# A delta-rule mixer: the chunk decay goes from the keys to the values, its state product becomes two half products on opposite rows, and the gate's projections are issued during the inversions

## The chip, the cores and the metric

The kernel runs on one core of a Trainium2 chip, in one launch. The figure of merit is the device time of one execution in microseconds (us); the median of the runs is given. Beside these times stands one profiled execution, whose trace gives the rows below.

## The reference, cut to what matters

A first block (mixer, then 32 experts) is followed by a second block. The change touches only the first block's mixer, which works on 256 context and 256 latent tokens of width 1024. It has a gated delta rule of 8 heads and a gated linear attention (GLA) of 4 heads, both run forwards and backwards:

```
def step(s, xs_n):                       # delta rule, chunks of 64 tokens
    u_n, w_n, attn_n, qg_n, kd_n, gl_n = xs_n
    v_new = u_n - w_n @ s
    o_n = qg_n @ s + attn_n @ v_new
    s = s * gl_n + kd_n^T @ v_new        # kd = k * exp(g[-1] - g)
    return s, o_n

ya = (rms_norm(o_a) * silu(za)) @ w_out_a      # za: columns 3072..4095 of the input projection
yb = (rms_norm(o_b) * silu(rb)) @ w_out_b
y  = (sigmoid(gates_a) * ya + sigmoid(gates_b) * yb) @ w_out
```

`u` and `w` come from a unit lower triangular system per chunk. `kd` scales every key row (token) of a chunk by its decay to the chunk's end. Since the product sums over tokens, the same factor may stand on the rows of `v_new`.

## The kernel before, in words

The mixer is `phase1`. Its program order around the change is written out as a string, `DELTA_ORDER` (L187), one letter for a piece of work: `K`, `Q`, `V` take a 128-column tile of keys, queries or values through projection, convolution and norm (`P` starts such a tile ahead); `M` forms the triangular systems of four heads; nine `X` are the steps of their inversion (`inverses`, L630 and L632: a product and a subtraction on VectorE per row, 31 rows); `H` prepares a head (`head_setup`); eight `S` scan a pair of heads (`scan_step`); `k`, `q`, `v` project GLA's keys, queries and values; `m` computes a part of the modulation (`fill_mod`, eight 1 MB pieces of `w_mod`). `GLA_ORDER` does the same behind it: there `S` forms a quarter of the delta branch's norm and gate, and `silu_cols` in it projects 256 columns of `za`. A scheduler then interleaves the engines' instructions by its own costs; each engine and each queue works through its list in order.

Forward and backward chunks share every tile: at step n the forward chunk `cf` sits on one half of the 128 rows (`rf`) and the backward chunk `cb` on the other (`rb`), and the halves swap with every step. Per head and step, `scan_step` does this:

- L717, L718: keys times state, two products of 64 rows of output, into the two halves of one PSUM tile; L720: `r`, on VectorE.
- L723: `vn`, the inverse times `r`.
- L725, L726: `vn` is copied by ScalarE into the two diagonal blocks of `vb`, a 128x256 tile whose other blocks GpSimd has set to zero (L701).
- L741: one product of the scaled keys `ks` with `vb`, 256 columns wide, so that each half of the rows meets only its own columns.
- L743, or L745 and L747: the new state of both directions.
- from step 4 on L730, L731, L733, L735 to L737: the outputs.

`ks` is made in `head_setup`: `scaled` (L694) multiplies the keys in token order by `eDL`, on GpSimd, as it multiplies the values by `Bt` on VectorE. Both are four instructions a head. Three of the buffers named `y` by the trace (pool `p1y`, three of them, 8 KB a partition) hold a pair's `TT`, `vs` and `ks`; the pieces of `w_mod` pass through the same three.

A projection (`proj_tm`) has its weights split into a high and a low part by ScalarE (L150) and VectorE (L151), and three fp32r products for each of the eight row tiles of the weight (L164). For `za` there are two token tiles of 256 columns per letter `S`, and VectorE reads each from PSUM (L880).

Of the kernel before, what the change touches and what calls it, by code (L numbers as in the profile page):

```python
# [9 lines left out]
F32 = mybir.dt.float32  # L10
# [3 lines left out]
ALU = mybir.AluOpType  # L14
# [178 lines left out]
def phase1(k, A, B):  # L193
# [28 lines left out]
    def chps():  # L222
        return ps.tile([128, 128], F32, name=k.nm("ch"), tag="ch", bufs=3)

# [310 lines left out]
    def fill_gv(h):  # L535
        t = wd.tile([128, 4, 256], F32, name=k.nm("gv"), tag="gv", bufs=2)
        proj_tm(w_in[:, 5152 + h * 256:5408 + h * 256], range(4), hTh, hTl, lambda i, o: nc.scalar.copy(t[:, i, :], o))
        gv.append(t)

    msc = k.dpool.tile([4, 1024], F32, name="msc")  # L540
    k.msc = msc

    def fill_mod(j):
        mp = ps.tile([128, 512], F32, name=k.nm("ch"), tag="ch", bufs=3)
# [8 lines left out]
    fills = {"k": fill_gk, "q": fill_gq, "v": fill_gv}  # L553

# [93 lines left out]

    def head_setup(h, TT, vs, ks):
        hh, h, (M, EA, Dn, Dt) = h, h % 4, groups[h // 4]  # L650
# [46 lines left out]
        comb(vs, scaled(nc.vector, vts[hh], Bt))  # L697
        comb(ks, scaled(nc.gpsimd, kt, eDL))
        st = wd.tile([128, 256], F32, name=k.nm("st"), tag="st", bufs=2)
        vb = wd.tile([128, 2, 256], F32, name=k.nm("vb"), tag="vb", bufs=2)  # L700
        nc.gpsimd.memset(vb, 0.0)  # L701
        os_ = wd.tile([128, 4, 128], F32, name=k.nm("os"), tag="os", bufs=2)
        return A2, TT, vs, ks, st, vb, os_

    def scan_step(p, n):
# [5 lines left out]
        for h in hs:  # L711
            A2, TT, vs, ks, st, vb, os_ = sets[h]
            if n == 0:
# [25 lines left out]
            if n < 7:  # L739
                pu = ps.tile([128, 256], F32, name=k.nm("pu"), tag="pu", bufs=1)  # L740
                nc.tensor.matmul(pu, ks[:, n, :], vq, start=True, stop=True)  # L741
                if n == 0:
                    nc.vector.tensor_copy(st, pu)  # L743
                else:
                    nc.vector.scalar_tensor_tensor(st[:, 0:128], st[:, 0:128], gl[:, h, cf:cf + 1],  # L745
                                                   pu[:, 0:128], op0=ALU.mult, op1=ALU.add)
                    nc.vector.scalar_tensor_tensor(st[:, 128:256], st[:, 128:256], gl[:, 8 + h, cb:cb + 1],  # L747
                                                   pu[:, 128:256], op0=ALU.mult, op1=ALU.add)
        if n < 7:
# [10 lines left out]
    for c in DELTA_ORDER:  # L760
# [8 lines left out]
        elif c in "KQV":  # L769
            ct = order.pop(0)  # L770
            x = conv_silu(ct)
            if c == "K":
                kT = wd.tile([128, 512], F32, name=k.nm("kT"), tag="kT", bufs=5)
                l2n(x, 512, kT, 0.0)
                kTs.append(kT)
            elif c == "Q":
                qT = wd.tile([128, 256], F32, name=k.nm("qT"), tag="qT", bufs=4)
                l2n(x, 256, qT, qbias)
                qTs.append(qT)
            else:  # L780
# [20 lines left out]
    def gla_gates(h, d):  # L801

        f = d == 0
        kT, qT = gk[h], gq[h]
        pz = ps.tile([128, 512], F32, name=k.nm("ch"), tag="ch", bufs=3)
        nc.tensor.matmul(pz, gw[32 * d:32 * d + 16, h * 128:(h + 1) * 128], lr[32 * d:32 * d + 16, :], start=True, stop=True)
        T2 = lambda nm, tag, b=2: (wd if tag == "kt" else wk).tile([128, 512], F32, name=k.nm(nm), tag=tag, bufs=b)
        z, l = T2("z", "acc"), T2("l", "e", 3)
# [60 lines left out]
        p1 = ps.tile([128, 256], F32, name=k.nm("pu"), tag="pu", bufs=1)  # L869
# [4 lines left out]
    def silu_cols(c0, dst, ccs=range(4)):  # L874

        for cc in ccs:
            def ev(t, o):
                d = dst[t - 2][:, cc * 256:cc * 256 + 256]
                x = wk.tile([128, 256], F32, name=k.nm("zx"), tag="Z", bufs=2)
                nc.vector.tensor_scalar_max(x, o, LOW)  # L880
                sigmoid(k, d, x)
                nc.vector.tensor_mul(d, x, d)
            proj_tm(w_in[:, c0 + cc * 256:c0 + cc * 256 + 256], (2, 3), hTh, hTl, ev)

# [65 lines left out]
    for c in GLA_ORDER:  # L950
# [1105 lines left out]
```

## Time and profile before

| | us |
|---|---|
| median of 3 runs | 2509.11 |
| lowest and highest | 2506.01, 2515.05 |
| the profiled execution | 2497.63 |
| its span on the core | 2495.8 |
| busy in it: PE (TensorE) | 2326.6 (93%) |
| busy: DVE (VectorE) | 1236.1 (50%) |
| busy: ACT (ScalarE) | 920.5 (37%) |
| busy: POOL (GpSimd) | 117.9 (5%) |

The page's 40 slices show three parts: the mixer up to about 745 us, the experts from 760 to 1700 us (DMA at nine tenths or more), and the second block to the end. The mixer's stages, read from the first and last starts of their lines: first inversion 107 to 176 us; scan of pair 0 to 222; its setup for pair 1 to 240; pair 1 to 285; second inversion and setup 300 to 367; pair 2 to 410; setup of pair 3 to 429; pair 3 to 467; GLA and the gates to 640; output projections and router to 745. A share of busy time over the whole span says little here: each stage has its own limit, so the windows by stage are the view to read.

### The profile page before, as it was taken

How to read it: one execution, taken by the hardware profiler on the slowest of the kernel's cores; microseconds unless marked ns; L12 is line 12 of the kernel's file. 1: busy time of each engine (PE TensorE's matmuls, PEld its weight loads, DVE VectorE, ACT ScalarE, POOL GpSimd, SP SyncE). 2: the span in 40 equal slices, each digit the busy share in tenths (PEclk: the TensorE clock that was granted, in tenths of full speed). 3: DMA queues.
4: the chain of work that ended last, by engine and by line, in shares of the span. 5: the costliest groups of instructions: out<-in, count | busy, mean ns of one | idle time of the engine just before them, and what ended most of it. 6: DMA issues, size and time to landing. Idle time of an engine off the chain costs nothing.

```text
span 2495.8 us, 36511 instructions
## 1 busy us (share of the span) xinstructions
PE 2326.6 (93%) x14474; PEld 1567.1 (63%) x14475; DVE 1236.1 (50%) x2717; ACT 920.5 (37%) x1956; POOL 117.9 (5%) x156
## 2 busy tenths in 40 slices
PE   6689879999989999999899999999999999999998
PEld 3476557889873433333334333336868999878998
DVE  4898897677560111112202121115766556766655
ACT  4556555577430101010101010104555445455544
POOL 0122122000010000000000000000010000010000
PEclk8899988999999999999999999999999999999999
DMA  8532330234889999999999999995335554524553
GB/s 285 139 85 60 133 97 26 60 94 120 283 297 380 415 416 416 416 416 416 389 416 415 416 415 416 416 415 150 112 85 173 170 171 155 159 73 138 186 186 102
DMA packets 290349, 605.90 MB, mean 243 GB/s; under 512 B 26038, under 2 KB 218681, under 8 KB 254332
## 3 DMA queue, kind: packets, MB, share of 16 engines
q1 hardware_dynamic: 283236, 595.24, 64.9%
q10 hardware_dynamic: 6280, 7.80, 1.2%
q8 instruction: 116, 1.90, 0.3%
q0 software_dynamic: 656, 0.46, 0.1%
q14 instruction: 61, 0.50, 0.1%
HBM read 602.30 MB, written 1.15 MB: 242 GB/s over the span
## 4 chain that ended last, share of the span: by engine, by line
PE 25%; issue 14%; DMA 9%; DVE 2%; ACT 1%; POOL 0%; SPq 0%; POOLq 0%; DVEq 0%; ACTq 0%
PE qm L164 13%; DMA w<-in_w_gu_dram 6%; PE yd L1373 2%; DMA w<-in_w_down_dram 2%; PE gt L1357 2%; PE lt L1357 2%; PE tr L1342 1%; PE qm L1789 0%; PE qm L1788 0%; PE ql L1852 0%; POOL bs L1805 0%; PE ql L1614 0%; PE tr L1286 0%; PE lt L1362 0%; PE gt L1362 0%
## 5 line engine op out<-in xcount | busy, mean ns | idle before, releaser
L150 ACT CAST wh<-w 128x1024 fp32r<-128x1024 f32 (+2 forms) x318 | 318.6, 1002 | 298.3 <-PE qm L164 201.2
L151 DVE TENSOR_TENSOR wl<-w,wh 128x1024 fp32r<-128x1024 f32 (+2 forms) x318 | 370.2, 1165 | 38.4 <-ACT wh L150 36.8
L1252 ACT ACTIVATE sg<-g 128x1024 f32<-128x1024 f32 x16 | 16.9, 1057 | 726.9 <-DVE g L1250 682.2
L164 PE MATMUL qm<-uh,wh 128*128 128x272 f32 (+2 forms) x1008 | 260.2, 292 | 0.0
L164 PE MATMUL qm<-ul,wh 128*128 128x272 f32 (+2 forms) x1008 | 258.3, 289 | 0.0
L1250 DVE TENSOR_SCALAR g<-gt 128x1024 f32<-128x1024 f32 x16 | 19.6, 1225 | 469.0 <-PE gt L1362 413.5
L1373 PE MATMUL yd<-w,aT 128*64 128x512 f32 x1024 | 228.3, 600 | 0.2 <-ACT aT L1264 0.2
L164 PEld LDWEIGHTS qm<-uh,wh 128*128 128x128 f32 (+1 forms) x1008 | 188.8, 188 | 7.4 <-issue 5.1
L164 PEld LDWEIGHTS qm<-ul,wh 128*128 128x128 f32 (+1 forms) x1008 | 189.3, 188 | 2.5 <-issue 0.7
L1357 PE MATMUL lt<-w,resB 128*64 128x512 f32 x512 | 189.6, 594 | 0.6 <-DVE act L1251 0.6
L1357 PE MATMUL lt<-w,xg 128*64 128x512 f32 x512 | 188.2, 596 | 0.0
L1357 PE MATMUL gt<-w,resB 128*64 128x512 f32 x512 | 182.6, 599 | 5.5 <-DMA w<-in_w_gu_dram 5.5
L1357 PE MATMUL gt<-w,xg 128*64 128x512 f32 x512 | 177.1, 602 | 8.5 <-DMA w<-in_w_gu_dram 8.3
L1373 PEld LDWEIGHTS yd<-w,aT 128*64 128x64 f32 x1024 | 72.9, 138 | 143.2 <-issue 140.8
L164 PE MATMUL qm<-uh,wl 128*128 128x272 f32 (+2 forms) x1008 | 147.7, 287 | 0.0
L1272 DVE TENSOR_TENSOR ys<-yd,g2r 128x512 f32<-128x512 f32 x32 | 20.6, 686 | 248.0 <-PE yd L1373 231.4
L164 PE MATMUL mm<-hTh,wh 128*128 128x256 f32 (+1 forms) x384 | 130.1, 358 | 8.3 <-ACT wh L150 4.1
L164 PEld LDWEIGHTS qm<-uh,wl 128*128 128x128 f32 (+1 forms) x1008 | 132.4, 187 | 0.7 <-issue 0.4
L164 PE MATMUL qm<-fl,wh 128*128 128x272 f32 (+1 forms) x512 | 128.6, 287 | 0.0
L164 PE MATMUL qm<-fh,wh 128*128 128x272 f32 (+1 forms) x512 | 128.4, 288 | 0.0
L164 PE MATMUL mm<-hTl,wh 128*128 128x256 f32 (+1 forms) x384 | 125.8, 347 | 0.0
L1357 PEld LDWEIGHTS lt<-w,xg 128*64 128x64 f32 x512 | 60.0, 138 | 71.4 <-issue 70.1
(581 smaller groups left out, 4392.7 us busy)
## 6 DMA issues: line engine op xcount, KB each, us to landing
w<-in_w_gu_dram SPq DMA_DIRECT2D x256, 1024.0 KB
w<-in_w_down_dram SPq DMA_DIRECT2D x128, 1024.0 KB
w<-in_w_ff_dram SPq DMA_DIRECT2D x64, 1024.0 KB
w<-in_w_in_dram SPq DMA_DIRECT2D x72, 512.0 KB
w<-in_w_in_dram SPq DMA_DIRECT2D x30, 1024.0 KB
y<-in_w_mod_dram SPq DMA_DIRECT2D x19, 1024.0 KB
w<-in_w_out_dram SPq DMA_DIRECT2D x24, 512.0 KB
w<-in_w_mod_dram SPq DMA_DIRECT2D x5, 1024.0 KB
```

The costliest lines, as they stand in the source:

```text
L150: k.nc.scalar.copy(hi, x)
L151: k.nc.vector.tensor_sub(lo, x, hi.bitcast(F32))
L164: nc.tensor.matmul(out, l, r, start=start and n == 1, stop=stop and n == 3 * len(terms))
L1250: nc.vector.tensor_scalar(g, gt, 7.0, LOW / 1.702, op0=ALU.min, op1=ALU.max)
L1252: nc.scalar.activation(sg, g, AF.Exp, scale=-1.702)
L1272: nc.vector.tensor_mul(ys[:, js], yd[:, js], g2r[:, js])
L1342: nc.tensor.matmul(o, hx[:, t, f * 128:(f + 1) * 128], S[t].rearrange("p e s -> p (e s)"), start=(t == 0 and i == 0), stop=(t == 1 and i = ...
L1357: nc.tensor.matmul(quarter(j)[64 * i:64 * i + 64], xg[:, kk, c0:c0 + CAP], w[i][:, j * 512:(j + 1) * 512], start=(kk == 0), stop=False)
L1373: nc.tensor.matmul(yd[64 * i:64 * i + 64, j * 512:(j + 1) * 512], aT[:, 2 * f2 + f, 64 * i:64 * i + 64], w[i][:, f, j * 512:(j + 1) * 512] ...
```

## The change

Part one moves the decay. `eDL` is combined once into `ceDL` (four VectorE copies), and `scan_step` writes the scaled `vn` in one ScalarE activation with a scale per row. `ks`, its 32 GpSimd products and the zeroing of `vb` go; at the last step, where no state follows, the copies go too.

Part two splits the state product by rows. The two halves of the keys `kt` and of `vq` are multiplied in two products over 64 rows each, into two PSUM tiles. `ch` has four buffers where it had three, and the tag `pu` goes.

Part three takes the four `za` projections out of GLA's `S` and gives them a letter of their own, `s`, after the third and sixth `X` of each inversion. Their result now holds one of the three `y` buffers from then on; a pair's setup needs two.

```diff
-DELTA_ORDER = "EkPPKPKPKPKMmXXXXXXXXXPQPQPVVHHkqSSSSSSSS...EkPPKPKPKPKMXXXXXXXXXPQPQPVmVHHSSSSSSSS..."
+DELTA_ORDER = "EkPPKPKPKPKMmXXXsXXXsXXXPQPQPVVHHkqSSSSSSSS...EkPPKPKPKPKMXXXsXXXsXXXPQPQPVmVHHSSSSSSSS..."
-        return ps.tile([128, 128], F32, name=k.nm("ch"), tag="ch", bufs=3)
+        return ps.tile([128, 128], F32, name=k.nm("ch"), tag="ch", bufs=4)
+    comb(ceDL, lambda r, d, q: nc.vector.tensor_copy(d, tv(eDL[:, :, 8 * q:8 * q + 8])[r]))
+    def fill_z(i):
+        if i == 0:
+            t = big([2, 1024])
+            z.extend(t[:, j, :] for j in range(2))
+        silu_cols(3072, z, (i,))
...
-        comb(ks, scaled(nc.gpsimd, kt, eDL))
-        vb = wd.tile([128, 2, 256], F32, name=k.nm("vb"), tag="vb", bufs=2)
-        nc.gpsimd.memset(vb, 0.0)
+        vb = wd.tile([128, 2, 128], F32, name=k.nm("vb"), tag="vb", bufs=2)
...
-            vq = vb[:, u]
-            nc.scalar.copy(vq[rf, 0:128], vn[rf])
-            nc.scalar.copy(vq[rb, 128:256], vn[rb])
+            if n < 7:
+                vq = vb[:, u]
+                nc.scalar.activation(vq, vn, AF.Copy, scale=ceDL[:, n, h:h + 1])
...
-                nc.tensor.matmul(pu, ks[:, n, :], vq, start=True, stop=True)
+                pu = chps(), chps()
+                nc.tensor.matmul(pu[0], kt[rf, cf // 2, :], vq[rf], start=True, stop=True)
+                nc.tensor.matmul(pu[1], kt[rb, cb // 2, :], vq[rb], start=True, stop=True)
...
-                trio = [big([2, 8, 128]) for _ in range(3)]
+                duo = [big([2, 8, 128]) for _ in range(2)]
-        G = T2("G", "kt")
+        G = T2("G", "vt")
-        p0 = ps.tile([128, 256], F32, name=k.nm("pu"), tag="pu", bufs=1)
+        p0 = ps.tile([128, 256], F32, name=k.nm("pu"), tag="ch", bufs=4)
...
             ba_.rms(2 * i, 2)
-            silu_cols(3072, z, (i,))
             ba_.columns(i)
```

TensorE's list in the scan of pair 3, before (`vb` the copied values, `y` the scaled keys, `st` the state, `kT` keys, `tm` a projection with weight parts `wh`, `wl`):

```order
L164 MATMUL tm_4540<-wh_4523,hTl 128x256
L164 MATMUL tm_4540<-wh_4523,hTh 128x256
L164 MATMUL tm_4540<-wh_4523,hTl 128x256
L735 MATMUL ch_4212<-vn_734_4210,A_680_3949 128x128
L741 MATMUL pu_4216<-vb_4021,y_677_3941 128x256
L717 MATMUL ch_4220<-st_4102,kT_2719 64x128
L718 MATMUL ch_4220<-st_4102,kT_2719 64x128
L164 MATMUL tm_4540<-wl_4524,hTh 128x256 x4
```

And in the scan of pair 3 of the changed kernel (`vb` the scaled values, `kt` the plain keys in token order):

```order
L164 MATMUL tm_4833<-wh_4829,hTh 128x256
L762 MATMUL ch_4454<-vb_4321,kt_4251 128x128
L763 MATMUL ch_4455<-vb_4321,kt_4251 128x128
L737 MATMUL ch_4460<-st_4397,kT_2875 64x128
L738 MATMUL ch_4460<-st_4397,kT_2875 64x128
L164 MATMUL tm_4833<-wh_4829,hTl 128x256
L164 MATMUL tm_4833<-wl_4830,hTh 128x256 x4
```

The wide product has become two neighbours of half its width, directly ahead of the other head's keys-times-state pair; that holds for 47 of the 56 state products.

VectorE's list near the end of the first inversion, before (`Ts`, `tmp` the inversion, `acc` a convolution tap, `wl` a weight's low part):

```order
L632 TENSOR_TENSOR Ts_969<-Ts_969,tmp_972 128x8x24
L151 TENSOR_TENSOR wl_1157<-w_1154,wh_1156 128x1024
L630 TENSOR_TENSOR tmp_972<-Ms_967,Ts_969 128x175
L501 SCALAR_TENSOR_TENSOR acc_1130<-pad_1127,cwT,acc_1130 128x256
L632 TENSOR_TENSOR Ts_969<-Ts_969,tmp_972 128x7x25
L515 TENSOR_TENSOR qT_1088<-e_1082,e_1089 128x256
L630 TENSOR_TENSOR tmp_972<-Ms_967,Ts_969 128x156
L501 SCALAR_TENSOR_TENSOR acc_1130<-pad_1127,cwT,acc_1130 128x256
L632 TENSOR_TENSOR Ts_969<-Ts_969,tmp_972 128x6x26
```

At the same rows of the inversion, changed (`zx` the evicted quarter of `za`, L652 and L654 the inversion):

```order
L654 TENSOR_TENSOR Ts_974<-Ts_974,tmp_977 128x8x24
L652 TENSOR_TENSOR tmp_977<-Ms_972,Ts_974 128x175
L151 TENSOR_TENSOR wl_1096<-w_1093,wh_1095 128x1024
L549 TENSOR_SCALAR zx_1057<-tm_1001 128x256
L654 TENSOR_TENSOR Ts_974<-Ts_974,tmp_977 128x7x25
L652 TENSOR_TENSOR tmp_977<-Ms_972,Ts_974 128x156
L654 TENSOR_TENSOR Ts_974<-Ts_974,tmp_977 128x6x26
L652 TENSOR_TENSOR tmp_977<-Ms_972,Ts_974 128x135
L654 TENSOR_TENSOR Ts_974<-Ts_974,tmp_977 128x5x27
L151 TENSOR_TENSOR wl_1128<-w_1125,wh_1127 128x1024
L551 TENSOR_TENSOR y_112_994<-zx_1057,y_112_994 128x256
```

The gate's work has taken the place of convolution taps (L501) between the inversion's rows; the taps stand later in the list.

GpSimd's list ahead of the scan of pair 3, before (`y` at L668 the tile `TT`, at L694 the scaled keys):

```order
L668 MEMSET y_675_3939 128x1024 x2
L701 MEMSET vb_4021 128x512
L654 MEMSET A_680_3949 128x512
L701 MEMSET vb_4103 128x512
L654 MEMSET A_692_4031 128x512
L694 TENSOR_TENSOR y_677_3941<-kt_3947,tok 64x4x128
L694 TENSOR_TENSOR y_677_3941<-kt_3947,tok 64x2x2x128
L694 TENSOR_TENSOR y_677_3941<-kt_3947,tok 64x4x128
```

And the same place, changed:

```order
L676 MEMSET A_759_4253 128x512
L690 MEMSET y_755_4244 128x1024 x2
L676 MEMSET A_771_4330 128x512
L879 MEMSET AT_4993 128x256
L879 MEMSET AT_5054 128x256
```

The products on the keys are gone from GpSimd's list, and GLA's zeroing (L879) follows at once.

## Rows read from the trace of the kernel before

**Rows 1.** Windows by stage: us, busy time and instructions per engine, granted clock, DMA share, GB/s.

```profile
107.00:176.00 69.00, 51.29 (x375) 39.70 (x367) 65.68 (x135) 35.85 (x78) 13.65 (x13) 0.90 0.39 108
176.00:222.00 46.00, 45.99 (x278) 32.85 (x278) 37.22 (x97) 27.20 (x76) 4.21 (x6) 0.97 0.16 47
...
300.00:367.00 67.00, 50.81 (x342) 32.64 (x341) 61.65 (x142) 31.45 (x72) 12.45 (x14) 0.87 0.37 119
410.00:429.00 19.00, 12.97 (x179) 10.09 (x179) 15.01 (x26) 13.18 (x49) 13.43 (x14) 0.71 0.01 2
429.00:467.00 38.00, 38.00 (x262) 30.23 (x261) 17.22 (x51) 14.33 (x46) 0.00 (x0) 0.97 0.15 42
467.00:640.00 173.00, 170.04 (x1245) 153.95 (x1245) 134.35 (x328) 124.41 (x309) 2.50 (x8) 1.00 0.40 115
...
760.00:1700.00 940.00, 879.80 (x3782) 341.23 (x3779) 165.44 (x238) 87.54 (x124) 1.09 (x2) 0.99 1.00 406
```

**Rows 2.** Windows, L164 on PE alone, in the GLA stage: us, busy, clock, DMA, GB/s.

```profile
467.00:640.00 173.00, 126.49 (x972) 1.00 0.40 115
```

**Rows 3.** Timeline of PE in the scan of pair 3: start, us, instruction, count.

```profile
454.74 0.28 PE L164 MATMUL tm<-wh,hTl 128*128 128x256 f32 x1
454.86 0.28 PE L164 MATMUL tm<-wh,hTh 128*128 128x256 f32 x1
...
456.35 0.59 PE L741 MATMUL pu<-vb,y 128*128 128x256 f32 x2
456.78 0.38 PE L735 MATMUL ch<-vn,A 128*128 128x128 f32 x2
457.10 0.32 PE L717 MATMUL ch<-st,kT 128*64 128x128 f32 x1
```

**Rows 4.** Timeline of PE in the second block, around products over 64 rows.

```profile
1731.97 0.29 PE L164 MATMUL qm<-uh,wh 128*128 128x272 f32 x1
1732.19 0.51 PE L1720 MATMUL ql<-ki,resA 64*128 64x144 f32 x2
1732.63 0.39 PE L164 MATMUL qm<-ul,wh 128*128 128x272 f32 x1
...
1736.24 0.52 PE L1720 MATMUL ql<-ki,resA 64*128 64x144 f32 x4
1736.69 0.39 PE L164 MATMUL qm<-uh,wh 128*128 128x272 f32 x1
```

**Rows 5.** One line's instructions, L694 on DVE: count, ns shortest/median/longest, first and last start.

```profile
L694 DVE TENSOR_TENSOR y<-vt,tok x32: 673/690/1541, 156.1 to 428.9; 64x512 f32<-64x512 f32 x32
```

**Rows 6.** Groups by shape, 60 to 480 us: busy us, mean ns; idle before, releasers.

```profile
L151 DVE TENSOR_TENSOR wl<-w,wh 128x1024 fp32r<-128x1024 f32 x36 | 43.8, 1217 | 5.1 <-ACT wh L150 3.8 <-PE mm L164 1.2
L694 POOL TENSOR_TENSOR y<-kt,tok 64x512 f32<-64x512 f32 x32 | 38.8, 1230 | 26.6 <-ACT kt L646 25.0 <-PE ch L723 1.0
...
L694 DVE TENSOR_TENSOR y<-vt,tok 64x512 f32<-64x512 f32 x32 | 30.9, 985 | 0.3
...
L726 ACT COPY vb<-ch 64x128 f32<-64x128 f32 x64 | 16.7, 260 | 0.8
...
L755 DVE TENSOR_TENSOR resB<-os 64x256 f32<-64x256 f32 x16 | 10.1, 633 | 0.2
```

**Rows 7.** Timeline of DVE in the setup of pair 3: start, us, instruction, count.

```profile
414.45 0.85 DVE L755 TENSOR_TENSOR resB<-os 64x256 f32<-64x256 f32 x2
...
417.00 1.44 DVE L694 TENSOR_TENSOR y<-vt,tok 64x512 f32<-64x512 f32 x1
418.36 2.45 DVE L755 TENSOR_TENSOR resB<-os 64x256 f32<-64x256 f32 x2
420.83 4.35 DVE L694 TENSOR_TENSOR y<-vt,tok 64x512 f32<-64x512 f32 x3
...
426.24 3.32 DVE L694 TENSOR_TENSOR y<-vt,tok 64x512 f32<-64x512 f32 x4
```

**Rows 8.** One line's instructions, L880: the eviction of the gate's projection.

```profile
L880 DVE TENSOR_SCALAR zx<-tm x16: 409/416/426, 478.5 to 620.4; 128x256 f32<-128x256 f32 x16
```

More of the change, by code (lines that the diff above doesn't have):

```diff
@@ L181, in parts @@
     return wh, wl
-DELTA_ORDER = "EkPPKPKPKPKMmXXXXXXXXXPQPQPVVHHkqSSSSSSSSPPQPQPVVHHSSSSSSSSEkPPKPKPKPKMXXXXXXXXXPQPQPVmVHHSSSSSSSSkPPQPQPVqqVHHSSSSSSSSqvv"
+DELTA_ORDER = "EkPPKPKPKPKMmXXXsXXXsXXXPQPQPVVHHkqSSSSSSSSPPQPQPVVHHSSSSSSSSEkPPKPKPKPKMXXXsXXXsXXXPQPQPVmVHHSSSSSSSSkPPQPQPVqqVHHSSSSSSSSqvv"
 GLA_ORDER = "DSGGGGOvDSGODGSORvDSRGRBBBGbORbbBbbbbb"
@@ L459, in phase1 @@
     ceG = one.tile([128, 8, 8], F32, name="ceG")
+    ceDL = one.tile([128, 8, 8], F32, name="ceDL")
     comb(cnbe, lambda r, d, q: nc.vector.tensor_copy(d, tv(nbe[:, :, 8 * q:8 * q + 8])[r]))
     comb(ceG, lambda r, d, q: nc.vector.tensor_copy(d, tv(eG[:, :, 8 * q:8 * q + 8])[r]))
+    comb(ceDL, lambda r, d, q: nc.vector.tensor_copy(d, tv(eDL[:, :, 8 * q:8 * q + 8])[r]))
     pcw = smps(216)
@@ L538, in fill_gv, with silu_cols, ev @@
         gv.append(t)
+    def silu_cols(c0, dst, ccs=range(4)):
+        for cc in ccs:
+            def ev(t, o):
+                d = dst[t - 2][:, cc * 256:cc * 256 + 256]
+                x = wk.tile([128, 256], F32, name=k.nm("zx"), tag="Z", bufs=2)
+                nc.vector.tensor_scalar_max(x, o, LOW)
+                sigmoid(k, d, x)
+                nc.vector.tensor_mul(d, x, d)
+            proj_tm(w_in[:, c0 + cc * 256:c0 + cc * 256 + 256], (2, 3), hTh, hTl, ev)
     msc = k.dpool.tile([4, 1024], F32, name="msc")
@@ L543, in fill_mod @@
     def fill_mod(j):
-        mp = ps.tile([128, 512], F32, name=k.nm("ch"), tag="ch", bufs=3)
+        mp = ps.tile([128, 512], F32, name=k.nm("ch"), tag="ch", bufs=4)
         for kk in range(8):
@@ L551, in fill_mod @@
                                 mo[32 * q:32 * q + 1, :])
-    fills = {"k": fill_gk, "q": fill_gq, "v": fill_gv}
+    z = []
+    def fill_z(i):
[3 more added lines that the diff above has]
+        silu_cols(3072, z, (i,))
+    fills = {"k": fill_gk, "q": fill_gq, "v": fill_gv, "s": fill_z}
     groups, kTs, qTs, vts, sets = {}, [], [], [], {}
@@ L647, in to_tok, with head_setup @@
         return vt
-    def head_setup(h, TT, vs, ks):
+    def head_setup(h, TT, vs):
         hh, h, (M, EA, Dn, Dt) = h, h % 4, groups[h // 4]
@@ L697, in head_setup @@
         comb(vs, scaled(nc.vector, vts[hh], Bt))
-        comb(ks, scaled(nc.gpsimd, kt, eDL))
         st = wd.tile([128, 256], F32, name=k.nm("st"), tag="st", bufs=2)
-        vb = wd.tile([128, 2, 256], F32, name=k.nm("vb"), tag="vb", bufs=2)
-        nc.gpsimd.memset(vb, 0.0)
+        vb = wd.tile([128, 2, 128], F32, name=k.nm("vb"), tag="vb", bufs=2)
         os_ = wd.tile([128, 4, 128], F32, name=k.nm("os"), tag="os", bufs=2)
-        return A2, TT, vs, ks, st, vb, os_
+        return A2, TT, vs, kt, st, vb, os_
     def scan_step(p, n):
@@ L711, in scan_step @@
         for h in hs:
-            A2, TT, vs, ks, st, vb, os_ = sets[h]
+            A2, TT, vs, kt, st, vb, os_ = sets[h]
             if n == 0:
@@ L739, in scan_step @@
             if n < 7:
-                pu = ps.tile([128, 256], F32, name=k.nm("pu"), tag="pu", bufs=1)
-                nc.tensor.matmul(pu, ks[:, n, :], vq, start=True, stop=True)
[L742 to L748, printed above, removed]
+                pu = chps(), chps()
+                nc.tensor.matmul(pu[0], kt[rf, cf // 2, :], vq[rf], start=True, stop=True)
+                nc.tensor.matmul(pu[1], kt[rb, cb // 2, :], vq[rb], start=True, stop=True)
+                for d, c in enumerate((cf, cb)):
+                    sd = st[:, 128 * d:128 * d + 128]
+                    if n == 0:
+                        nc.vector.tensor_copy(sd, pu[d])
+                    else:
+                        nc.vector.scalar_tensor_tensor(sd, sd, gl[:, 8 * d + h, c:c + 1], pu[d], op0=ALU.mult, op1=ALU.add)
         if n < 7:
@@ L787, in phase1 @@
             if i % 2 == 0:
-                trio = [big([2, 8, 128]) for _ in range(3)]
-            sets[i] = head_setup(i, *(x[:, i % 2] for x in trio))
+                duo = [big([2, 8, 128]) for _ in range(2)]
+            sets[i] = head_setup(i, *(x[:, i % 2] for x in duo))
         elif c == "S":
@@ L804, in gla_gates @@
         kT, qT = gk[h], gq[h]
-        pz = ps.tile([128, 512], F32, name=k.nm("ch"), tag="ch", bufs=3)
+        pz = ps.tile([128, 512], F32, name=k.nm("ch"), tag="ch", bufs=4)
         nc.tensor.matmul(pz, gw[32 * d:32 * d + 16, h * 128:(h + 1) * 128], lr[32 * d:32 * d + 16, :], start=True, stop=True)
-        T2 = lambda nm, tag, b=2: (wd if tag == "kt" else wk).tile([128, 512], F32, name=k.nm(nm), tag=tag, bufs=b)
+        T2 = lambda nm, tag, b=2: (wd if tag == "vt" else wk).tile([128, 512], F32, name=k.nm(nm), tag=tag, bufs=b)
         z, l = T2("z", "acc"), T2("l", "e", 3)
@@ L868, in gla_gates @@
         nc.scalar.copy(ss_[:, 0, :], p0)
-        p1 = ps.tile([128, 256], F32, name=k.nm("pu"), tag="pu", bufs=1)
+        p1 = ps.tile([128, 256], F32, name=k.nm("pu"), tag="ch", bufs=4)
         nc.tensor.matmul(p1, kdt[:, 2, :], gv[h][:, 2 + fi, :], start=True, stop=True)
@@ L872, in gla_gates @@
         return qs, AT, ss_
[L874 to L883, printed above, removed]
     def gate_cols(base, dst, tiles=range(8)):
@@ L930, in columns @@
                                                op0=ALU.mult, op1=ALU.subtract)
-    z, ga = big([2, 1024]), big([8, 256])
-    z, ga = [z[:, t, :] for t in range(2)], [ga[:, i, :] for i in range(8)]
+    ga = big([8, 256])
+    ga = [ga[:, i, :] for i in range(8)]
     ba_ = Branch(oa, 8, z, 32, Halves(wk, k, "g4", 2), Halves(wk, k, "s16", 2))
@@ L1039, in ev_out @@
         return fn
-    pl = [ps.tile([128, 32], F32, name=k.nm("pl"), tag="ch", bufs=3) for _ in range(2)]
+    pl = [ps.tile([128, 32], F32, name=k.nm("pl"), tag="ch", bufs=4) for _ in range(2)]
     def logits(cc):
```

## The prediction, made before the changed kernel ran

> **What bounds the kernel now.** I read the slices of the page first: three parts, of which only the mixer (to 745 us) holds edited code. The window over the experts shows DMA busy for 1.00 of 940 us at 406 GB/s [rows 1], and the second block is unchanged. Both start from what the mixer hands over, so I count a microsecond saved in the mixer as one saved in all, and nothing saved behind it.
>
> Next came the windows by stage [rows 1]. They show three kinds. In the inversions (107 to 176, 300 to 367) DVE is busy for 65.68 of 69 and 61.65 of 67 us, while PE leaves 17.7 and 16.2 us idle: DVE sets the time. In the scans (176 to 222, 429 to 467) PE is busy throughout, 45.99 of 46 and 38.00 of 38, and DVE leaves 8.8 us in the first. In the GLA stage PE is busy for 170.04 of 173 us against 134.35 on DVE, and 126.49 of it are projections [rows 2]. So the same microsecond of PE costs nothing in an inversion and a whole one in the GLA stage, and a microsecond of DVE the reverse. The setup before pair 3 (410 to 429) is short of either: its path is a chain, and 13.43 of its 19 us have GpSimd busy.
>
> Third were the shapes of L694 and what DVE does beside it [rows 5 to 7].
>
> **The change part by part.** Terms are on the profiled execution, 2497.63 us.
>
> *GpSimd's products go.* They are 32 of 1230 ns, 38.8 us on GpSimd [rows 6]. GpSimd's own time I leave out: the setup of pair 3 ends with DVE's products (426.24 + 3.32, so 429.56 [rows 7]), not with GpSimd. What counts is DVE beside them. L694 on DVE takes 690 ns in the median and 673 at the least, but 985 in the mean [rows 5, 6]: 32 x (985 - 690) = 9.4 us lost. L755 takes 0.85 us for two when undisturbed and 2.45 in the midst of it [rows 7], 633 ns in the mean [rows 6] against 425: 16 x 0.208 = 3.3. Together 12.7 us. Other DVE operations must meet the same products, so the true relief is larger: if all 38.8 us took from DVE what L755 lost at 418.36 (1.225 against 0.425, 65%), it would be 25. Against that, part of it lies where a chain waits for PE or ACT. In the setup of pair 3 it can be followed [rows 7]: eight products take 1.44 + 4.35 + 3.32 = 9.1 us where 8 x 0.69 = 5.5 would do, and the L755 pair loses 1.6, so up to 5.2 us of that stretch. I take the 12.7 that rows show, -13, with -25 and -5 as ends.
>
> The Trainium skill would have it larger for each meeting ("SBUF — State Buffer", Who interferes with whom): a DVE instruction with both inputs in SBUF and a GpSimd one that reads SBUF exclude each other, and the loser waits the whole instruction. By that, some 15 disturbed products at 1.2 us each would give 18 us where the means give 9.4. The longest L694 on DVE, 1541 ns against 690 [rows 5], is 0.85 over: less than a whole GpSimd product. I stay with the means.
>
> *The gate's projections in the inversions.* A quarter costs DVE two weight splits of 1.217 [rows 6], two evictions of 0.416 [rows 8] and two multiplications that I price alike: 4.1 us, four quarters 16.4. The inversions are where DVE is full. But the order shows that convolution taps left the inversion's last rows for later in the list, and behind it come the scans, where DVE idles 8.8 of 46 us. About half should be absorbed: +9, from 0 to +16. On PE a quarter is 2 x 8 x 3 = 48 products, and those follow each other by 0.12 us (454.74 to 454.86, [rows 3]): 192 x 0.12 = 23 us, against 33.9 us of idle PE in the two inversions. Hidden there; if the evictions come late it is not, which is the slow rival below.
>
> *The same work out of the GLA stage.* PE loses 23 of its 170 us, DVE 16.4 of 134, so PE is still the bound (147 against 118). The 3 us that PE idles now stay: -22. From below, DVE or a chain of ScalarE takes over halfway, -11; from above, some waits at evictions go as well, -27.
>
> *The state product in two halves.* Before, L741 stands 0.43 us (456.35 to 456.78, [rows 3]). There is no such product over 64 rows in the mixer, but there is one in the second block: L1720, a 64-row product of 144 columns. One (x2 records) takes 0.44 us to the next start, two (x4) take 0.45 (1736.24 to 1736.69, [rows 4]): the two lie beside each other at no added time. From the projected end of the neighbour before it (1731.97 + 0.12) to the start of the one behind (1732.63) are 0.54 us. Its entry alone is 0.10 (1732.09 to 1732.19), and I take its exit alike, which leaves 0.34 for the product, 0.30 at 128 columns. In 47 of 56 places the next instruction is L717, a product over the columns' halves, whose own entry was paid before too. So the pair costs 0.10 + 0.30 = 0.40 against 0.43 there, and 0.50 against 0.43 in the nine others: 47 x -0.03 + 9 x 0.07 = -0.8. The state update is two small copies for one at n = 0 and waits on two PSUM tiles of a pool that is now shared: I take +1 in all. Ends: -3, and +12 if the halves run one after the other (0.22 each, 56 times).
>
> The Trainium skill speaks against this part ("TensorEngine Tiling (Array Packing)", Key Properties): a change of tiling mode drains TensorE. One more change per state product, 56 in all, would be 5.6 us by the 0.10 of the row. The row agrees that a change costs, but the narrower product gives 0.13 back, so the sum doesn't move.
>
> *One activation for two copies.* L725 and L726 are 0.26 each [rows 6], one behind the other, between the inverse's product and the state product. One activation over 128 rows lies between 0.26 and 0.52; at 0.35 a head-step is 0.17 shorter. In the scans PE is full with projections beside the chain, so most is hidden: -2, from 0 to -9 (56 x 0.17).
>
> *One `y` buffer held by the gate.* In the second half the pieces of `w_mod` pass through two buffers, not three. DMA's share in 300 to 367 is 0.37 [rows 1], so there is room; eight pieces of 1 MB at 406 GB/s are 2.6 us each, of which one or two can be late and hold up weights queued behind them on SP: +1, from 0 to +8.
>
> The four copies for `ceDL`, the fourth `ch` buffer and the other tags I cost at nothing: DVE has slack where the copies stand, at the start; without it they are under 2 us.
>
> Sum: -13 + 9 - 22 + 1 - 2 + 1 = -26, so 2471.6 us beside the profiled 2497.63. That execution stands 11.5 us under the median of 2509.11; from the median it is 2483.
>
> **The rivals.** *B: the GLA stage gives only half.* DVE is busy for 134 of 173 us there and ScalarE for 124; with PE at 147, their chains (the gates' logarithms, the splits of weights) may set the end, -11 in place of -22: 2494. For it: two other engines are within 30% of the bound. Against: PE idles 3 us in 173.
>
> *C: the halves do not run beside each other*, +12 in place of +1: 2494. For it: L1720 is in another place, with other neighbours. Against: x4 takes what x2 takes [rows 4].
>
> *D: no relief on DVE*, because what L694 loses is lost behind other waits: the -13 is 0, 2496. Against: DVE is 95% busy in the first inversion [rows 1].
>
> *E, the slow one: the gate's eviction holds up the inversion.* The evicted tile `zx` shares two buffers with the inversion's `tmp`, one of which is held throughout, and both PSUM buffers of projections are taken until it is done. Per quarter the chain of max, three activations and multiplication would stop the key and query projections for some 4.5 us: 4 x 4.5 = 18, with all 16 of DVE on the path, +34 where I have +9, and half of the relief lost, +7. That is -26 + 25 + 7 = +6, and up to +14 with the pieces of `w_mod` 8 us late as well; the middle is +10, about 2519. For it: one free buffer, in-order engines. Against: PE has 34 us of slack. It decides if the scan of pair 0 starts later than about 13 us after the 176 of now.
>
> **How the numbers follow.** Forecast 0.56, with its own range 2470 to 2492; B 0.18; C 0.10; D 0.08; E 0.08. The bounds of the terms reach 2466 below (relief and GLA at their ends); above, B, C and D lie at 2494 to 2496 and together with one more small miss at 2503. A measurement of this kernel tells about 0.3% (7.5 us) from no change. Faster by more than that (under 2501.6): nearly all of the forecast and most of B, C and D, 0.82. Within: the rest of these, 0.11. Slower: E's most, 0.07.
>
> **What would show it.** In the changed profile L694's like on GpSimd is absent, and on DVE its mean falls to about 0.69. The scan of pair 0 starts between 172 and 182 us. The setup before pair 3 falls from 19 to about 14 us. From the end of pair 3 to the output projections it takes about 151 us where it took 173, PE still nearly without idle time. The two half products start together and occupy about 0.4 us. The forecast is wrong if the inversions grow by more than 16 us, if the GLA stage keeps more than 162 us, or if the halves start 0.2 us apart.

## The result, and the profile after

The changed kernel takes 2527.9 us in the median (2526.99 to 2529.78, 4 runs) against 2507.56 for the kernel before (2504.96 to 2515.05, 4 runs): a ratio of 1.0067, 95% interval 1.004 to 1.0094. The forecast was 2483, range 2466 to 2503. The kernel became slower by 20 us, which the text had given 7 in 100.

Stages, in us, each bounded by the first start or the last end of a line in the traces. The profiled execution of before stands 10 us under the median, so a second profile of it (the run e7 below) stands beside it:

| | first inversion to scan of pair 0 | pairs 0, 1 | second inversion to pair 2 | pairs 2, 3 | GLA, to the first output projection | to the first expert product |
|---|---|---|---|---|---|---|
| before | 63.9 | 122.1 | 71.2 | 110.9 | 171.3 | 95.8 |
| before, second profile | 65.0 | 123.5 | 71.3 | 113.1 | 173.1 | 92.8 |
| after | 73.5 | 121.9 | 69.0 | 114.3 | 193.7 | 93.8 |

The GLA stage, forecast to shrink by 22 us, grew by 21 to 22; the first inversion grew by 9 to 10. The second inversion is 2 us shorter, and the other stages move by at most 3.4 us, where the two profiles of before differ by up to 3.0. The windows of the changed kernel over these six stages, with the columns of [rows 1]:

```profile
106.00:180.00 74.00, 56.78 (x410) 46.42 (x402) 69.30 (x141) 41.26 (x87) 4.03 (x5) 0.88 0.45 129
180.00:301.00 121.00, 115.55 (x936) 81.08 (x936) 94.78 (x239) 71.16 (x173) 10.40 (x15) 0.93 0.25 61
301.00:371.00 70.00, 56.95 (x458) 41.37 (x457) 62.58 (x148) 36.20 (x79) 5.04 (x7) 0.85 0.53 168
371.00:485.00 114.00, 112.86 (x972) 88.15 (x971) 72.71 (x198) 59.27 (x180) 4.74 (x8) 0.96 0.19 52
485.00:678.00 193.00, 160.15 (x1001) 136.15 (x1000) 115.64 (x283) 105.27 (x249) 4.23 (x7) 0.88 0.29 80
678.00:772.00 94.00, 82.98 (x646) 80.35 (x645) 58.68 (x128) 35.71 (x59) 11.04 (x18) 0.93 0.95 329
```

In the fifth row no engine is full any more: PE idles 33 us of 193, DVE and ACT are busy for 60% or less, and DMA for 0.29. That looks like a chain with nothing beside it. The waits of PE in that stage name it (total us, times, longest):

```profile
PE ch L882 <- DVE qk L855: 27.2, 8, 5.8
PE sm L875 <- DVE kd L871: 1.7, 2, 0.9
PE pu L888 <- ACT kdt L877: 1.7, 3, 0.6
```

L882 is GLA's attention product; its first one for each head and direction waits here, eight times in all. It stands at the end of a chain that begins with L827, the gate's product `pz`, and goes over VectorE and ScalarE to the scaled queries and keys `qk`. PE's timeline of the changed kernel over one and a half such chains (of the projections behind the first row 16 are left out):

```profile
526.71 1.12 PE L827 MATMUL ch<-lr,gw 16*128 16x512 f32 x2
...
529.73 1.09 PE L164 MATMUL mm<-hTh,wl 128*128 128x256 f32 x8
536.58 0.80 PE L882 MATMUL ch<-qk 128*128 128x128 f32 x2 [5.75 <-DVE qk L855]
...
538.85 0.90 PE L875 MATMUL sm<-cst,kd 128*128 128x128 f32 x3
540.32 2.07 PE L888 MATMUL pu<-gv,kdt 128*128 128x256 f32 x4 [0.57 <-ACT kdt L877]
542.19 1.06 PE L891 MATMUL pu<-gv,kdt 128*128 128x256 f32 x2
543.17 1.29 PE L827 MATMUL ch<-lr,gw 16*128 16x512 f32 x2
...
545.79 0.59 PE L957 MATMUL mm<-gv,AT 128*128 128x256 f32 x2
551.52 0.77 PE L882 MATMUL ch<-qk 128*128 128x128 f32 x2 [5.13 <-DVE qk L855]
```

And the same place in the kernel before, where L806 is the gate's product, L861 the attention product, L854 the transposes, L867 and L870 the state products:

```profile
494.87 0.68 PE L861 MATMUL ch<-qk 128*128 128x128 f32 x4 [0.59 <-DVE qk L834]
495.48 0.45 PE L862 MATMUL ch<-off 128*64 128x64 f32 x4
495.86 1.12 PE L806 MATMUL ch<-lr,gw 16*128 16x512 f32 x2
...
497.44 0.49 PE L854 MATMUL sm<-cst,kd 128*128 128x128 f32 x3
...
498.64 1.03 PE L867 MATMUL pu<-gv,kdt 128*128 128x256 f32 x4
...
500.14 0.70 PE L870 MATMUL pu<-gv,kdt 128*128 128x256 f32 x2
```

Before, the next direction's gate product follows the attention products at once (495.86), and the transposes and state products of the direction at hand are done while the next chain already runs on the other engines. After, the gate product stands behind all of them (543.17, 6.6 us after the attention product at 536.58), and the next chain starts only then. That is so in all of the chains. Two things had changed at that place, and both could do it: the `za` projections, which used to stand in the gaps, were gone; and the state products' PSUM had moved from a tag of its own (`pu`) into `ch`, which the gate product and the attention products use too. (The gates' tile `G` had also gone from the tag `kt` to `vt`, and `ch` had a fourth buffer; neither is so in e1 below.)

### The profile page after: what moved, and what is told of

It reads as the page before. It is cut to its first block, busy times and chain, and to the rows that moved or that the text cites. A ratio compares the mean times of both kernels' runs of the same rounds, so it can differ in the third digit from the quotient of the medians.

```text
span 2525.2 us, 36568 instructions
## 1 busy us (share of the span) xinstructions
PE 2341.2 (93%) x14586; PEld 1574.2 (62%) x14587; DVE 1220.4 (48%) x2729; ACT 906.5 (36%) x1884; POOL 75.3 (3%) x116
## 4 chain that ended last, share of the span: by engine, by line
PE 23%; issue 14%; DMA 10%; DVE 2%; ACT 1%; POOL 0%; SPq 0%; POOLq 0%; DVEq 0%; ACTq 0%
PE qm L164 13%; DMA w<-in_w_gu_dram 8%; DMA w<-in_w_down_dram 2%; PE yd L1382 2%; PE gt L1366 2%; PE lt L1366 1%; PE tr L1351 1%; PE qm L1798 0%; PE qm L1797 0%; PE ql L1861 0%; POOL bs L1814 0%; PE ql L1623 0%; PE tr L1295 0%; PE ql L1816 0%; PE lt L1371 0%
## 5 line engine op out<-in xcount | busy, mean ns | idle before, releaser
L164 PE MATMUL qm<-uh,wh 128*128 128x272 f32 (+2 forms) x1008 | 260.4, 292 | 0.0
L164 PE MATMUL qm<-ul,wh 128*128 128x272 f32 (+2 forms) x1008 | 258.5, 289 | 0.0
L164 PEld LDWEIGHTS qm<-uh,wh 128*128 128x128 f32 (+1 forms) x1008 | 188.9, 188 | 7.4 <-issue 5.1
L164 PEld LDWEIGHTS qm<-ul,wh 128*128 128x128 f32 (+1 forms) x1008 | 189.4, 188 | 2.5 <-issue 0.7
L1366 PE MATMUL gt<-w,xg 128*64 128x512 f32 x512 | 175.6, 598 | 6.6 <-DMA w<-in_w_gu_dram 6.5
L164 PE MATMUL qm<-uh,wl 128*128 128x272 f32 (+2 forms) x1008 | 147.7, 286 | 0.0
L164 PEld LDWEIGHTS qm<-uh,wl 128*128 128x128 f32 (+1 forms) x1008 | 132.4, 187 | 0.7 <-issue 0.4
L164 PE MATMUL qm<-fl,wh 128*128 128x272 f32 (+1 forms) x512 | 128.6, 286 | 0.0
L164 PE MATMUL qm<-fh,wh 128*128 128x272 f32 (+1 forms) x512 | 128.4, 288 | 0.0
L164 PE MATMUL mm<-hTh,wh 128*128 128x256 f32 (+1 forms) x384 | 124.5, 345 | 0.7 <-DVE zx L549 0.6
L164 PE MATMUL mm<-hTl,wh 128*128 128x256 f32 (+1 forms) x384 | 123.4, 342 | 0.0
L1366 PEld LDWEIGHTS lt<-w,resB 128*64 128x64 f32 x512 | 57.8, 137 | 74.7 <-issue 72.4
```

The source lines that it names most:

```text
L164: nc.tensor.matmul(out, l, r, start=start and n == 1, stop=stop and n == 3 * len(terms))
L1366: nc.tensor.matmul(quarter(j)[64 * i:64 * i + 64], xg[:, kk, c0:c0 + CAP], w[i][:, j * 512:(j + 1) * 512], start=(kk == 0), stop=False)
```

## The experiments

Two theories: *lost filler* (the chains were always this long, `za` covered them) and *shared buffers* (a `ch` buffer that the next gate product needs is not free until the direction at hand is through). The first four runs cross the two.

**e1: the kernel before, with GLA's two state tiles in `ch`.**

```diff
-        p0 = ps.tile([128, 256], F32, name=k.nm("pu"), tag="pu", bufs=1)
+        p0 = ps.tile([128, 256], F32, name=k.nm("pu"), tag="ch", bufs=3)
...
-        p1 = ps.tile([128, 256], F32, name=k.nm("pu"), tag="pu", bufs=1)
+        p1 = ps.tile([128, 256], F32, name=k.nm("pu"), tag="ch", bufs=3)
```

> The kernel before, with one edit: the GLA branch's two state tiles p0 and p1 take their PSUM from the tag ch (three buffers, shared with the gate product pz and the attention products pa) instead of the tag pu of their own. Theory 'shared buffers': in the changed kernel the GLA stage grew because pz of the next direction now waits for a ch buffer that the current direction still uses, so the 10 us gate chains of successive directions no longer overlap. It expects the GLA stage (end of pair 3 to first output projection, 171 us before) at 185 to 200 and the total at 2522 to 2537. Theory 'lost filler': the stage grew because the za projections that stood between a gate chain's start and its end are gone; they are here, so it expects 171 us and 2508 within 5.

2532.8 us, ratio 1.0102 (1.0074 to 1.013); GLA stage 198.6 us. Two tags alone make the kernel before slower than the change did, with every `za` product in its old place. Ahead of GLA its lists are those of before, instruction for instruction, yet that part took 9 us longer in its profile than in the first profile of before: so much can single executions differ. PE's waits in the GLA stage of this run; before had 2.8 us in 6 times in the first of these:

```profile
PE ch L861 <- DVE qk L834: 15.3, 8, 5.1
PE sm L854 <- DVE kd L850: 3.5, 4, 0.9
```

**e2: the changed kernel, with these tiles in `sm`.**

```diff
-        p0 = ps.tile([128, 256], F32, name=k.nm("pu"), tag="ch", bufs=4)
+        p0 = smps(256)
...
-        p1 = ps.tile([128, 256], F32, name=k.nm("pu"), tag="ch", bufs=4)
+        p1 = smps(256)
```

> The changed kernel, with p0 and p1 of the GLA branch in the tag sm (two buffers) instead of ch; all else of the change stays. 'Shared buffers' expects the GLA stage to fall from 194 us to 145 to 165 (the projections that left it are 23 us) and the total to 2483 to 2500. 'Lost filler' expects no more than a few us: stage above 185, total 2520 to 2530.

2501.0 us, ratio 0.9982 (0.997 to 0.9994); GLA stage 166.4 us, 27 less. Shared buffers holds on both kernels, from either side. The timeline of PE shows the old order again, the gate product (L827) right behind the attention products:

```profile
492.56 0.44 PE L883 MATMUL ch<-off 128*64 128x64 f32 x4
492.93 1.12 PE L827 MATMUL ch<-lr,gw 16*128 16x512 f32 x2
493.99 0.55 PE L875 MATMUL sm<-cst,kd 128*128 128x128 f32 x3
495.10 2.08 PE L888 MATMUL sm<-gv,kdt 128*128 128x256 f32 x4 [0.57 <-ACT kdt L877]
```

But 166 is not 150: taking `za` out gave the stage only some 7 us.

**e3 and e4: `za` back in the GLA stage**, with the tiles in `ch` (e3) and in `sm` (e4).

```diff
-DELTA_ORDER = "...MmXXXsXXXsXXX...KMXXXsXXXsXXX..."
+DELTA_ORDER = "...MmXXXXXXXXX...KMXXXXXXXXX..."
...
             ba_.rms(2 * i, 2)
+            silu_cols(3072, z, (i,))
             ba_.columns(i)
```

> The changed kernel with the za projections back in the GLA stage (the letter s gone, silu_cols in S as before); the decay on the values, the half products and the tags as changed. 'Lost filler' expects the GLA stage back at 171 us and a total of 2490 to 2502 (what the first two parts gain). 'Shared buffers' expects the stage at 190 us or more, since filler does not undo the order, and the total at 2515 to 2530.

> The changed kernel with the za projections back in the GLA stage and p0 and p1 in sm: the decay on the values and the half products alone, without the two suspects. Both theories expect the GLA stage at 165 to 173 us. By the prediction's terms (-13 relief of VectorE, +1 products, -2 ScalarE) the total is about 2494; if the relief is not on the path, 2507. Against the run with the za projections early and sm, it prices the early projections: +9 in the inversions and -22 in the GLA stage were forecast.

e3: 2522.4 us, ratio 1.006 (1.0043 to 1.0078), GLA stage 199.5; filler alone does not undo it, and the tag by itself is again worth 26 us of the stage (e3 against e4). e4: 2493.1 us, ratio 0.9954 (0.9936 to 0.9972), GLA stage 173.0: the decay and the half products by themselves gain 11 to 14 us, against the -14 of the prediction's terms. Since e2 is slower than e4, the early `za` cost some 7 us net, where -13 was forecast.

**e5: e2 with the projections that are left spread between the chains.** Between gate product and attention product e2's list has 0, 6, 18 and 24 projection products in four of the eight chains; here one chain has none and the others have 42 or more. (The expectation's count of three empty chains is wrong, and the letters that ran are those of the diff.)

```diff
-GLA_ORDER = "DSGGGGOvDSGODGSORvDSRGRBBBGbORbbBbbbbb"
+GLA_ORDER = "DSSGGROvDSSGGRODGGRORvDGGbbObbBBBBbbbb"
```

> As the run with the early za projections and p0, p1 in sm (2501 us, GLA stage 166 us), but with GLA_ORDER rewritten so that the projections that are left stand between the gate chains: DSSGGROvDSSGGRODGGRORvDGGbbObBBBBBbbbb in place of DSGGGGOvDSGODGSORvDSRGRBBBGbORbbBbbbbb. In that run three of the eight chains have no projection product between their start and their end in TensorE's list, here one. Theory 'lost filler is the rest': with the shared buffers out of the way, the stage is set by chains that nothing covers; it expects 145 to 155 us and a total of 2481 to 2491. Theory 'another engine': VectorE or ScalarE sets the stage at about 165 us however the projections stand; total 2497 to 2505.

2490.7 us, ratio 0.9944 (0.9926 to 0.9962); GLA stage 152.3 us. PE is nearly full again, as this window over the stage shows, and DVE's 115 and ACT's 108 us are no bound:

```profile
488.00:640.00 152.00, 143.65 (x1000) 127.88 (x999) 115.36 (x289) 107.74 (x260) 1.87 (x6) 0.97 0.37 103
```

So in e2 lost filler was real, as a second layer below the first: 14 us of it. With both mended, the stage gives 173.0 - 152.3 = 20.7 us for `za`, against 22 forecast; the two orders differ, but PE idles about as long in both (7.5 us in e4, 8.4 in e5). This is the fastest of the versions, a little ahead of e4 with intervals that overlap; both beat both kernels.

**e6: e4 plus the 32 products on GpSimd**, into a third `y` buffer per pair, which nothing reads.

```diff
         comb(vs, scaled(nc.vector, vts[hh], Bt))
+        comb(ks, scaled(nc.gpsimd, kt, eDL))
...
-                duo = [big([2, 8, 128]) for _ in range(2)]
+                duo = [big([2, 8, 128]) for _ in range(3)]
```

> As the run with the za projections back and p0, p1 in sm (2493 us), plus the 32 GpSimd products of the keys with eDL into a third y buffer, which nothing reads: the removed cost by itself, put back. The prediction's term (relief of VectorE 13 us, 5 to 25) expects 2506, and 2498 to 2518 as ends; the VectorE products of the values should be at 0.9 to 1.0 us in the mean again, against 0.69. If the relief is off the path, 2493 within 4.

2506.4 us, ratio 0.9999 (0.9981 to 1.0017): 13.3 us more than e4 by the medians, 11 by the ratios. The groups by shape of e6 and then of e4 (busy us, mean ns), the products on VectorE and on GpSimd:

```profile
L716 POOL TENSOR_TENSOR y<-kt,tok 64x512 f32<-64x512 f32 x32 | 38.5, 1220 | 29.3 <-ACT kt L668 28.6
L716 DVE TENSOR_TENSOR y<-vt,tok 64x512 f32<-64x512 f32 x32 | 31.2, 998 | 0.4
```

```profile
L716 DVE TENSOR_TENSOR y<-vt,tok 64x512 f32<-64x512 f32 x32 | 21.1, 683 | 0.8 <-ACT vt L668 0.5
```

The relief is of the size of the prediction's first term (-13). The run has a rival of its own: the third `y` buffer is taken again as well, and the modulation's pieces pass through these buffers. From the first product of pair 0's scan to the second inversion's first instruction the two can be told apart. Windows of e6 and of e4 over that stretch, with the columns of [rows 1]:

```profile
170.55:301.49 130.94, 120.97 (x1040) 82.88 (x1037) 108.59 (x252) 72.78 (x176) 24.89 (x28) 0.95 0.26 69
174.50:296.08 121.58, 116.32 (x1037) 82.04 (x1034) 99.61 (x246) 69.68 (x161) 9.22 (x15) 0.96 0.31 78
```

With the products the stretch is 9.4 us longer and VectorE busy for 9.0 us more, with nearly the same instructions; its idle time is the same (22.4 and 22.0 us). So the loss there is VectorE's own time; a wait for a buffer would have shown as idle time. The kernel before has the same picture (129.7 us, VectorE busy for 108.5). By the stages of the table the difference shows up later: 9.4 us in the second inversion (69.9 against 60.5), of which 6.8 are there at the first row of the inversion, 34 us ahead of the stage's first GpSimd product, and 6.5 in pairs 2 and 3. How the rest divides between products and buffer was not separated. The first inversion is 3.6 us shorter with the products, but its list is another one: VectorE has 126 instructions there against 133.

**e7: the kernel before, profiled again.**

> The kernel before, a second profile. The profiled execution of before stands 9 us below the median, and a run whose lists are the same as before's up to the GLA stage spent 9 us more ahead of it. If that is the spread between executions, this profile has its end of pair 3 later than the 475.0 us of the first profile by up to 10 us, with a lower granted clock in the first inversion; if the first profile is typical, within 2 us.

2509.3 us; counted from the first inversion's start, pair 3 ends 4.7 us later, and the granted clock in 107 to 176 us is 0.85 against 0.90 of [rows 1]. The first profile was a quick one, by half of the 10 us that I allowed.

**What early `za` costs: e8 to e12.** It holds a `y` buffer, so the second fill of the modulation passes through two. In e4 seven of its pieces are issued in one run of the SP queue; in e5 they come in small groups, with the last four at 335, and the weights behind them at 351 (timelines of SP, e4 and then e5, from the runs of pieces on). PE waits 5.4 us for pieces in e5's second inversion and 0.8 in e4's.

```profile
290.76 21.14 SPq L250 DMA_DIRECT2D y<-in_w_mod_dram  x7
327.55 25.54 SPq L171 DMA_DIRECT2D w<-in_w_in_dram  x6
```

```profile
...
305.95 1.01 SPq L250 DMA_DIRECT2D y<-in_w_mod_dram  x1
318.81 2.38 SPq L171 DMA_DIRECT2D w<-in_w_in_dram  x2
322.61 0.34 SPq L250 DMA_DIRECT2D y<-in_w_mod_dram  x1
331.64 0.37 SPq L171 DMA_DIRECT2D w<-in_w_in_dram  x1
335.48 10.68 SPq L250 DMA_DIRECT2D y<-in_w_mod_dram  x4
351.21 19.45 SPq L171 DMA_DIRECT2D w<-in_w_in_dram  x4
```

e8 puts that fill behind the first, ahead of `za`; e11 and e12 put it behind pair 3's scan, with `za` early (e11, on e5) and late (e12, on e4). e9 instead makes the low parts of `za`'s weights on GpSimd; e10 is e8 and e9 together.
The edits of e8, of e11 (and e12), and of e9 (`eng` is GpSimd for `za`, nothing elsewhere):

```diff
-DELTA_ORDER = "...KMmXXXsXXXsXXX...PQPQPVmVHH..."
+DELTA_ORDER = "...KMmmXXXsXXXsXXX...PQPQPVVHH..."
```

```diff
-DELTA_ORDER = "...PQPQPVmVHH...qqVHHSSSSSSSSqvv"
+DELTA_ORDER = "...PQPQPVVHH...qqVHHSSSSSSSSmqvv"
```

```diff
-    k.nc.vector.tensor_sub(lo, x, hi.bitcast(F32))
+    (eng or k.nc.vector).tensor_sub(lo, x, hi.bitcast(F32))
```

> As the run with the spread filler (2491 us), but the second fill of the modulation stands right behind the first (KMmm...), before the za tile takes its y buffer, so its eight 1 MB pieces pass through three buffers and not two, and not in the second inversion. Theory 'pieces': in the second inversion with early za TensorE waited 13.6 us for these pieces and VectorE idled 7 of 69 us against 3 of 60 without; it expects the second inversion (end of pair 1 to start of pair 2, 71.6 us) at 66 to 68 and the total at 2484 to 2488. Theory 'VectorE alone': the growth is the 16 us that za costs VectorE; it expects 71 us there and the total within 2 us of 2491, or above it if the pieces now hold up the first inversion.

> As the run with the spread filler (2491 us), but the low parts of za's weights (eight subtractions of 128x1024, 1.22 us each on VectorE) are made by GpSimd, which has been free since its products went. If the inversions are VectorE's, 9.7 us leave them; what two-input work of GpSimd took from VectorE in the spare-products run (13.3 us for 38.5, a third) comes back for some 8 x 2.4 us, 6.6: total 2484 to 2490, about 2488. If the inversions are set by something else, 2491 to 2500 (the interference without the gain).

> Both edits of the two runs before it at once (second fill of the modulation early, za's low parts on GpSimd). If each has its own part of the time, their gains add: 2481 to 2486. If they share the same wait, no better than the better one of the two.

> As the run with the spread filler (2491 us, za early), but the second fill of the modulation stands behind the scan of pair 3, in a stage where two y buffers are free and DMA's share is under 0.4. Putting it into the first inversion took 9 us from the second inversion and gave 11 to the first. Theory 'pieces': with early za the pieces pass through two buffers and their waits lie on the second inversion's path; out of both inversions, its 71.6 us fall to 61 to 65, of which the GLA stage gives back 2 to 4: total 2481 to 2487. Theory 'VectorE alone': 70 us there and 2489 to 2495.

> As the run with the za projections back in the GLA stage and p0, p1 in sm (2493 us), with the second fill of the modulation behind the scan of pair 3. There the pieces had three buffers and the second inversion took 60.5 us. If the pieces cost time only because za holds a buffer, it stays at 58 to 61 and the total at 2491 to 2497 (GLA is TensorE's and takes the fill's products on top, some 3 us). If the fill itself costs the inversion several us whatever the buffers, it falls to 52 to 56 and the total to 2485 to 2490.

| | us | ratio (95%) | first inversion | second inversion | GLA |
|---|---|---|---|---|---|
| e4, `za` late | 2493.1 | 0.9954 (0.9936-0.9972) | 67.4 | 60.5 | 173.0 |
| e12, `za` late, fill late | 2524.7 | 1.0087 (1.0071-1.0103) | 66.3 | 60.2 | 202.2 |
| e5, `za` early | 2490.7 | 0.9944 (0.9926-0.9962) | 73.6 | 71.6 | 152.3 |
| e11, `za` early, fill late | 2520.5 | 1.0068 (1.0053-1.0083) | 73.2 | 59.4 | 189.1 |
| e8, `za` early, both fills first | 2501.0 | 0.9979 (0.9966-0.9993) | 84.5 | 62.5 | 156.1 |
| e9, e5 with GpSimd's low parts | 2492.0 | 0.9948 (0.993-0.9965) | 76.3 | 69.6 | 155.2 |
| e10, e8 and e9 | 2504.2 | 0.999 (0.9977-1.0004) | 86.4 | 65.4 | 153.3 |

As versions e8, e10, e11 and e12 are misses, by far in the late ones: there the GLA stage grows by 37 and 29 us, where I had allowed 2 to 4. PE waits for pieces at its start, 10.8 us in e11 and 4.5 in e12, and the granted clock is 0.61 in the first 43 us of e11's stage; the rest of the growth was not taken apart. As measurements of the second inversion e11 and e12 answer the question, by one profile each. With three buffers the fill costs it nothing (60.5 with, 60.2 without); with two it costs 12 us (71.6 with, 59.4 without); and once the fill is away, early `za` costs the second inversion nothing (59.4 against 60.2). What remains is the first inversion, 6 to 7 us longer with early `za` in each pair of rows. e8 moves the cost into the first inversion (+11 there, where PE waits 13.6 us for pieces against 3.3 in e5, and -9 in the second). The 13.6 us in e8's expectation are another number: PE's 5.4 us in e2's second inversion and the weight loader's 8.2, which overlap, so that PE waited 5.4. e9 does not move the time either way: whether VectorE's 9.7 us were won and lost again to interference is not resolved.

## Why the prediction was wrong, point by point

The change is +0.67%. By the ratios it is made of three parts: the decay and the half products, -0.46% (e4); early `za`, +0.28% (e2 against e4); the shared PSUM tag, +0.85% (after against e2), 21 us, 27 by the medians.

- **The step that failed: "the other tags I cost at nothing".** The move of `p0` and `p1` into `ch` costs 21 to 27 us. The cost is not in the scan, where I had allowed for a shared pool, but in the order that it forces on PE in the GLA stage: the gate product of the next chain stands behind the state products of the last, and PE waits 27.2 us for `qk` where e2 waits 10.5. The lists of both kernels show it; I had read them at the places of the three announced parts, and not in the GLA stage, on which my largest term rested.
- **"PE is still the bound (147 against 118)", -22.** PE's own sum was right: e5 takes 152.3. It only becomes the bound if the list leaves it something to do during each chain. Removed work was also cover, 14 of the 21 us in e2. Rival B had about the size of this loss (11 of the 22), for the wrong reason: neither VectorE nor ScalarE was near its limit. That it came near is luck.
- **The gate's projections in the inversions, +9.** Measured 6 to 7 us in the first inversion and none in the second. Hidden on PE, as forecast: it still idles 17 of the 74 us. The slow rival, their eviction holding up the inversion, did not come about: the scan of pair 0 starts 6 us later at its first state copy (181.2 us, 175.6 before), inside the interval given; at its first product it is 9 us later (179.6, 170.7).
- **The `y` buffer held by the gate, +1 (0 to +8).** The mechanism was right, pieces through two buffers with weights queued behind them, and the size was not: 12 us (e5 against e11). I had priced DMA's time, with a share that left room. What the runs show is late issue: the last four pieces of e5 leave at 335 and the weights behind them at 351. Why the queue reaches them so late was not taken apart.
- **GpSimd's products, -13.** 11 to 13 for e6 as a whole, of which 9 are seen as VectorE's own time. L716 on VectorE now takes 684 ns in the median and 692 at the most, against 1541 of [rows 5]. The prediction's "some 15" disturbed products are 12 in the trace of before, 1.40 to 1.54 us each. The 18 us by the rule of the Trainium skill ("SBUF — State Buffer", Who interferes with whom) stay above what the products lost (31.2 - 21.1 = 10.1 us in e6), and so would the 14 us that 12 products give.
- **The state product, +1.** PE's part was right: from the start of the pair to the next instruction it is 0.42 us in the median of the 56 places of e4, against 0.40 or 0.50 forecast and 0.43 before. The wait on two tiles, which made up the +1, was not separated. The halves start together, so rival C falls (PE's timeline of the changed kernel):

```profile
477.28 0.38 PE L755 MATMUL ch<-vn,A 128*128 128x128 f32 x2
477.60 0.37 PE L762 MATMUL ch<-vb,kt 64*128 64x128 f32 x1
477.60 0.37 PE L763 MATMUL ch<-vb,kt 64*128 64x128 f32 x1
...
478.02 0.61 PE L164 MATMUL mm<-hTh,wl 128*128 128x256 f32 x3
```

- **One activation for two copies, -2.** It takes 367 ns, where I had chosen 350 between 260 and 520. Its own share of the time was not separated; e4 as a whole agrees with the three terms' -14.
- **The signs.** Of the prediction's signs these came true: the start of pair 0, 684 ns on VectorE, halves that start together, and the setup of pair 3, from the last state product of pair 2 to the first of pair 3 (13.1 us, 19.1 before). Pairs 2 and 3 are not shorter for it. The one that called the forecast wrong is the GLA stage, 193.7 us where more than 162 was the limit.

## What to carry to other kernels

A buffer's tag is an edge in the order of work: when a tile moves to another tag, look in every stage that draws on either tag at what now stands ahead of what, and above all at the stage on which the forecast rests. Work that is taken from a full engine saves its time only where the rest still covers the chains of the other engines; count the cover per chain, not per stage. And a buffer lent for longer is priced by the loads that rotate through what is left, with the queue behind them, not by the bandwidth.

## What the runs showed of the hardware that was not expected

Where PE waited it was slow as well. In 540 to 580 us of the changed kernel, with PE busy for 28.22 of 40 us, the granted clock is 0.71 of full speed in the mean, so part of that time at the lower of its two levels (1.2 of 2.4 GHz), against 1.00 in the GLA stage of [rows 1], where PE hardly waited. L888, the same state product, takes 631 ns in the median of its records, and 379 before; at 540.32 four records take 2.07 us, where L867 took 1.03 at 498.64. So the exposed chain cost its wait and then part of the work behind it.

```profile
540.00:580.00 40.00, 28.22 (x94) 18.88 (x95) 19.76 (x54) 14.95 (x34) 0.62 (x2) 0.71 0.05 13
```

Beside the 32 two-input products of GpSimd (38.5 us in e6), VectorE's own 32 products take 31.2 us instead of 21.1, and the kernel 11 to 13 us more, about a third of GpSimd's time.
